# Query norms ahead of the turn, the causal mask as a product, and scores in two rings of banks

## The chip, the cores and the metric

One Trainium2 chip, one core of it. The metric is the device time of one launch in microseconds (us). Engines: PE is TensorE (matrix products into PSUM banks), DVE is VectorE, ACT is ScalarE, POOL is GpSimd, and SP issues most of the transfers.

## The reference

One transformer block on 256 tokens of width 2048, fp32 throughout. What matters here is the mixer's attention half: 8 query heads of 128 in 2 groups, each group sharing one key and value head.

```python
q = rope(rms_norm(q.reshape(B, S, NSA_HEADS, dh), q_norm_g), pos)
...
p_c = masked_softmax(jnp.einsum('bgsrd,bgcd->bgsrc', q, kc) * scale, mask_c)      # compressed, 15 blocks
...
p = masked_softmax(jnp.einsum('bgqrd,bgqkd->bgqrk', q_i, kg) * scale, mask)       # selected
...
p_w = masked_softmax(jnp.einsum('bgnqrd,bgnkd->bgnqrk', qw, kband) * scale, mask_w)  # window
...
return gates[..., 0:1] * o_cmp + gates[..., 1:2] * o_slc + gates[..., 2:3] * o_win
```

At 256 tokens there are four blocks to select from and 16 may be selected, and the window is 512 long, so the selected and the window branch are both plain causal attention, with keys of their own. The other half of the mixer is a gated linear recurrence (`rglru_branch`); after the mixer come an output projection and a PEER feed-forward that reads all 16384 experts.

## The kernel before

The kernel runs in three parts. The first (up to about 205 us) computes the modulation rows and most of the input projection. The second (about 205 to 365 us) finishes the projection and does the whole mixer. The third is the output projection (to 475 us) and the feed-forward (to the end).

All weights are streamed through four buffers of 1 MB (`raw`); each piece is split into a high and a low fp32r half (`split`: ACT line 209 casts, DVE line 210 subtracts), and three fp32r products stand for one fp32 product (`mm3`, lines 358 to 360). Besides, DVE works off rows of the modulation weights (`ada`, line 231, tile `av`, two buffers of 1 MB while the mixer runs), and PE takes others of them as products (`adp_item`, line 271).

The second part is a set of Python generators, `PROG` (line 57), that `mix` steps in turn: `q`/`e` evacuate a projected block (`ev_q`, `ev_kv`, `ev_rnn`), `b` and `l` are projection blocks (tiles `r` and `xg`), `c` is the compression, `r0` to `r3` are the four groups of the recurrence, `s0` to `s3` are the scores of group g = i // 2 and token block tb = i % 2, and `o0` to `o3` the outputs. The order in the program is a priority: a scheduler places each instruction in its engine's queue, and each engine then runs its queue in order.

`scores` works on one head a step, with n = 128 keys for tb = 0 and 256 for tb = 1, both branches side by side in one PSUM bank. PE makes two fp32 products (line 811). DVE scales by the query's norm out of PSUM into the tile `pt` (line 802, tb = 1 only, the part without mask), scales and masks the diagonal part (line 803), and takes the row maximum (line 806). ACT takes the exponential in place in `pt` and sums it (line 795). The score bank is free after lines 802 and 803. The norms `rq` come from `ev_q`, which turns the unnormed queries at once (line 641) and works out the norm beside that (lines 642, 643).

PSUM has one ring of four banks (`ps_x`, also called `PO`: projection blocks and attention outputs), one of three (`ps_t`, also `ps_a`: transposes, scores, recurrence gates) and one of one bank. The recurrence keeps one set of tiles `u`, `ta`, `ti`; PE's gates `rp` (line 756) wait for the convolution on DVE (line 751).

Of the kernel before, what the change touches and what calls it, by code (L numbers as in the profile page):

```python
# [7 lines left out]
F32 = mybir.dt.float32  # L8
F32R = mybir.dt.float32r
U32 = mybir.dt.uint32  # L10
I32 = mybir.dt.int32
AF = mybir.ActivationFunctionType
OP = mybir.AluOpType
AX = mybir.AxisListType

P = 128
# [3 lines left out]
NT = S // P  # L20
HD = 128
NH = 8
NG = 2
# [39 lines left out]
SCALE = HD ** -0.5  # L63
# [7 lines left out]
def kernel(  # L71
# [40 lines left out]
    ps_a = ps_t  # L112
    PO = ps_x
# [470 lines left out]
    kT = zp.tile([P, 2, NG, S], F32, name="kT")  # L584
    vv = zp.tile([P, NT, 2, NG, HD], F32, name="vv")
    gates = zp.tile([P, NT, 24], F32, name="gates")
    rq = zp.tile([P, NT, NH], F32, name="rq")
    kcT = zp.tile([P, 32], F32, name="kcT")
    vc = zp.tile([16, NG, HD], F32, name="vc")

    win = oT.rearrange("p h t -> p (h t)").rearrange("p (a l g n) -> p a l g n", a=2, l=32, g=2)
    ckT = xgT.rearrange("p h t -> p (h t)")[:, 0:4 * S].rearrange("p (a g t) -> p a g t", a=2, g=2)
    V.memset(win[:, :, :, :, NCMP:16], 0.0)
# [29 lines left out]
    def transpose4(zr, name):  # L623
        tp = ps_t(f"tp_{name}")
        for h in range(4):
            T.transpose(tp[:, h * P:(h + 1) * P], zr[:, h * P:(h + 1) * P], ident)
        return tp
# [4 lines left out]
    def ev_q(j, pst):  # L632
        tab = table(0)
        s = tp1.tile([P, NT, 4], F32, tag="ssq", bufs=2, name=f"ssq{j}")
        z = []
        for tb in range(NT):
            z.append(zrow(tp1, f"q{j}{tb}"))
            sumsq(s[:, tb], pst[tb], 4, f"q{j}{tb}")
            rope(z[tb], pst[tb], 4, tab[:, tb, 0], tab[:, tb, 1], f"q{j}{tb}")
            yield  # L640
        tp = transpose4(z[0], f"q{j}0")
        r = rsqrt(tp1, s.rearrange("p b h -> p (b h)"), HD, 8, f"q{j}")
        V.tensor_scalar(rq[:, :, 4 * j:4 * j + 4], r.rearrange("p (b h) -> p b h", b=NT), SCALE, None, OP.mult)
        yield
        A.copy(qT[:, 4 * j:4 * j + 4, tbs[0]], tp.rearrange("p (h t) -> p h t", h=4))
        tp = transpose4(z[1], f"q{j}1")
        yield
        A.copy(qT[:, 4 * j:4 * j + 4, tbs[1]], tp.rearrange("p (h t) -> p h t", h=4))
# [90 lines left out]
    def recurrence(gr):  # L739
        n = RG  # L740
        if True:
# [18 lines left out]
                A.activation(ta[:, c_], ta[:, c_], AF.Tanh, scale=spl[:, k:k + 1], bias=spl[:, k:k + 1])  # L760

            d = xr[:, :, 0:S]
            V.tensor_scalar(d, d, 0.5, 0.5, OP.mult, OP.add)
            V.scalar_tensor_tensor(out=u, in0=ti, scalar=1.0, in1=u, op0=OP.add, op1=OP.mult)
            yield
            V.scalar_tensor_tensor(out=ti, in0=ta, scalar=1.0, in1=d, op0=OP.add, op1=OP.mult)
            A.activation(ta, ta, AF.Sqrt)
            yield
            V.scalar_tensor_tensor(out=d, in0=ti, scalar=2.0, in1=d, op0=OP.subtract, op1=OP.mult)
            V.tensor_scalar(ti, d, -2.0, -1.0, OP.mult, OP.add)  # L770
            yield
            V.tensor_tensor(u, u, d, OP.mult)
            yield
            V.scalar_tensor_tensor(out=u, in0=ta, scalar=-1.0, in1=u, op0=OP.mult, op1=OP.mult)
            yield
            for i in range(n):
                V.tensor_tensor_scan(d[:, i], ti[:, i], u[:, i], 0.0, OP.mult, OP.add)
# [5 lines left out]
    def scores(sp, g, tb):  # L783

        n = (tb + 1) * P
        sums = sp.tile([P, 4, 2], F32, tag=f"sums{tb}", bufs=1, name=f"sums{tb}{g}")
        pts = [sp.tile([P, 2, n], F32, tag=f"pt{tb}", bufs=4, name=f"pt{tb}{g}{hh}") for hh in range(4)]
        m2 = sp.tile([P, 4, 2], F32, tag=f"m2{tb}", bufs=1, name=f"m2{tb}{g}")
        held[g, tb] = sums, pts
        scs = {}  # L790
        for i in range(6):
            if 0 <= i - 2:
                hh = i - 2
                for br in range(2):
                    A.activation(pts[hh][:, br], pts[hh][:, br], AF.Exp, bias=m2[:, hh, br:br + 1],
                                 accum_out=sums[:, hh, br:br + 1])
            if 0 <= i - 1 < 4:
                hh = i - 1
                s3 = scs.pop(hh)[:, 0:2 * n].rearrange("p (b n) -> p b n", b=2)
                r1 = rq[:, tb, 4 * g + hh:4 * g + hh + 1]  # L800
                if tb == 1:
                    V.tensor_scalar(pts[hh][:, :, 0:P], s3[:, :, 0:P], r1, None, OP.mult)
                V.scalar_tensor_tensor(
                    out=pts[hh][:, :, n - P:n], in0=s3[:, :, n - P:n], scalar=r1,
                    in1=caus.unsqueeze(1).to_broadcast([P, 2, P]), op0=OP.mult, op1=OP.add)
                V.tensor_reduce(m2[:, hh], pts[hh], AX.X, OP.max, negate=True)
            if i < 4:
                h = 4 * g + i
                scs[i] = ps_a(f"sc{tb}{h}")
                for br in range(2):  # L810
                    T.matmul(scs[i][:, br * n:(br + 1) * n], qT[:, h, tbs[tb]], kT[:, br, g, 0:n], start=True, stop=True)
            yield

    def outputs(sp, g, tb):
# [12 lines left out]
        for hh in range(4):  # L827
# [3 lines left out]
        cm = con[:, C_CMP + 16 * tb:C_CMP + 16 * tb + 16].unsqueeze(1).to_broadcast([P, 4, 16])  # L831
        va = con[:, C_VAL + 16 * tb:C_VAL + 16 * tb + 16].unsqueeze(1).to_broadcast([P, 4, 16])
        mx = sp.tile([P, 4], F32, tag="cmx", bufs=2, name=f"cmx{g}{tb}")
        V.tensor_tensor(pc, cps[:, 0:64].rearrange("p (h n) -> p h n", h=4),
                        rq[:, tb, hs].unsqueeze(2).to_broadcast([P, 4, 16]), OP.mult)
        V.tensor_tensor(pc, pc, cm, OP.add)
        V.tensor_reduce(mx, pc, AX.X, OP.max)
        V.tensor_tensor(pc, pc, mx.unsqueeze(2).to_broadcast([P, 4, 16]), OP.subtract)
        A.activation(pc, pc, AF.Exp)
# [600 lines left out]
```

## Time and profile before

| | us |
|---|---|
| median of 3 runs | 2024.65 (2024.57 to 2025.96) |
| the profiled execution | 2027.09 |
| its span in the trace | 2025.3 |
| PE busy in the span | 1953.6 (96%) |
| DVE busy | 1529.3 (76%) |
| ACT busy | 1024.1 (51%) |

The profiled execution took 1.8 us more than its span and 2.4 us more than the median. The shares are means over parts with different limits: after 475 us PE is busy all the time, before that it is not.

### The profile page before, as it was taken

To read this page: it belongs to the slowest core of one execution; us is meant where nothing else is said; L and a number is where in the kernel's file an instruction comes from. 1 tells how busy PE (TensorE), PEld (TensorE's weight loads), DVE (VectorE), ACT (ScalarE), POOL (GpSimd) and SP (SyncE) were. 2 spreads that over 40 slices of the span, in tenths; PEclk is the share of its full clock that TensorE was granted. 3 is DMA by queue.
4 is the path that set the end of the run, shared out by engine and by line. 5 is a ranking of instruction groups with operands and counts; after the bars stand their busy time and mean duration, and the time that the engine had idled before them with its cause. 6 is when DMAs were issued, how large, how long until landed. Compare 5 with 4: busy or idle time off the path is not lost.

```text
span 2025.3 us, 30935 instructions
## 1 busy us (share of the span) xinstructions
PE 1953.6 (96%) x12346; PEld 1728.4 (85%) x12346; DVE 1529.3 (76%) x2342; ACT 1024.1 (51%) x1519; POOL 67.6 (3%) x107
## 2 busy tenths in 40 slices
PE   5999898898999999999999999999999999999998
PEld 4777565787999999999998888888899999999997
DVE  7888999887999888788757666666566666665566
ACT  3544676455445767677654444444344444444442
POOL 0000000000000000000011000000000000000000
PEclk7999998898999999999999999999999999999999
DMA  9898778895546676666798776775577777676563
GB/s 374 325 372 330 277 307 315 345 347 219 175 169 208 215 260 234 229 230 232 270 331 300 246 242 229 234 251 201 190 267 253 262 250 253 240 243 212 190 223 131
DMA packets 77600, 515.39 MB, mean 254 GB/s; under 512 B 8720, under 2 KB 9232, under 8 KB 21904
## 3 DMA queue, kind: packets, MB, share of 16 engines
q1 hardware_dynamic: 63792, 450.50, 62.0%
q0 software_dynamic: 13664, 62.92, 9.0%
q8 instruction: 96, 1.57, 0.3%
q14 instruction: 48, 0.39, 0.1%
HBM read 481.93 MB, written 31.46 MB: 253 GB/s over the span
## 4 chain that ended last, share of the span: by engine, by line
PE 75%; DVE 10%; issue 10%; DMA 3%; ACT 2%; POOL 1%; SPq 0%; DVEq 0%; POOLq 0%
PE u L359 11%; PE u L358 11%; PE u L360 11%; PE d L377 8%; PE d L376 8%; PE d L375 8%; DVE av L231 3%; DVE wl L210 3%; PE wq L375 2%; PE wq L376 2%; PE wq L377 2%; PE y L360 1%; PE y L358 1%; PE y L359 1%; DMA wd<-stg 1%
## 5 line engine op out<-in xcount | busy, mean ns | idle before, releaser
L210 DVE TENSOR_TENSOR wl<-raw,wh 128x1024 fp32r<-128x1024 f32 x649 | 789.3, 1220 | 374.7 <-ACT wh L209 372.0
L209 ACT CAST wh<-raw 128x1024 fp32r<-128x1024 f32 x649 | 680.2, 1051 | 768.5 <-PE u L360 364.2
L377 PE MATMUL d<-xH,wl 128*128 128x256 f32 x2048 | 568.4, 278 | 0.8 <-DVE wl L210 0.7
L375 PE MATMUL d<-xH,wh 128*128 128x256 f32 x2048 | 568.4, 278 | 0.0
L376 PE MATMUL d<-xL,wh 128*128 128x256 f32 x2048 | 567.9, 277 | 0.0
L359 PE MATMUL u<-wl,ah 128*128 128x512 f32 x1024 | 398.9, 390 | 1.3 <-DVE wl L210 1.3
L358 PE MATMUL u<-wh,ah 128*128 128x512 f32 x1024 | 398.7, 389 | 0.0
L360 PE MATMUL u<-wh,al 128*128 128x512 f32 x1024 | 398.4, 389 | 0.0
L377 PEld LDWEIGHTS d<-xH,wl 128*128 128x128 f32 x2048 | 385.3, 188 | 1.3 <-DVE wl L210 1.2
L376 PEld LDWEIGHTS d<-xL,wh 128*128 128x128 f32 x2048 | 385.2, 188 | 0.4
L375 PEld LDWEIGHTS d<-xH,wh 128*128 128x128 f32 x2048 | 385.2, 188 | 0.4
L359 PEld LDWEIGHTS u<-wl,ah 128*128 128x128 f32 x1024 | 192.2, 188 | 41.2 <-DVE wl L210 1.7
L360 PEld LDWEIGHTS u<-wh,al 128*128 128x128 f32 x1024 | 192.3, 188 | 40.2
L358 PEld LDWEIGHTS u<-wh,ah 128*128 128x128 f32 x1024 | 192.2, 188 | 39.7
L231 DVE SCALAR_TENSOR_TENSOR av<-av,cb 128x2048 f32<-128x2048 f32 x64 | 145.8, 2283 | 6.0 <-DMA av<-in_ada_w_dram 6.0
L1198 DVE TENSOR_TENSOR oh<-con,idT 128x1024 fp32r<-128x1024 f32 x64 | 78.1, 1221 | 33.4 <-PE w L1218 33.3
L1228 ACT ACTIVATE ga<-oh,gh 128x128 fp32r<-128x128 f32 x256 | 83.0, 394 | 18.1 <-DVE oh L1198 16.3
L375 PE MATMUL wq<-xH,wh 128*128 128x256 f32 x256 | 73.5, 288 | 2.5 <-ACT xH L209 2.5
L376 PE MATMUL wq<-xL,wh 128*128 128x256 f32 x256 | 73.2, 286 | 0.0
L377 PE MATMUL wq<-xH,wl 128*128 128x256 f32 x256 | 73.0, 285 | 0.0
L1284 DVE TENSOR_TENSOR acc<-acc,u 128x512 f32<-128x512 f32 x112 | 71.5, 679 | 0.0
L1210 DVE TENSOR_TENSOR stg<-stg,w 128x256 f32<-128x256 f32 x128 | 48.3, 421 | 10.3 <-ACT stg L1209 10.3
(363 smaller groups left out, 2080.0 us busy)
## 6 DMA issues: line engine op xcount, KB each, us to landing
raw<-in_down_dram SPq DMA_DIRECT2D x128, 1024.0 KB, 5.6
raw<-in_up_dram SPq DMA_DIRECT2D x128, 1024.0 KB, 5.4
av<-in_ada_w_dram SPq DMA_DIRECT2D x64, 1024.0 KB, 7.1
raw<-in_w_a_dram SPq DMA_DIRECT2D x32, 1024.0 KB, 9.0
raw<-in_ada_p_dram SPq DMA_DIRECT2D x16, 1024.0 KB, 7.1
raw<-in_w_out_dram SPq DMA_DIRECT2D x16, 1024.0 KB, 8.1
raw<-in_wq_dram SPq DMA_DIRECT2D x16, 1024.0 KB, 5.2
wd<-stg POOLq DMA_DIRECT2D x8, 2048.0 KB, 8.4
```

The costliest lines, as they stand in the source:

```text
L209: A.copy(dst_h, src)
L210: V.tensor_tensor(dst_l, src, dst_h.bitcast(F32), OP.subtract)
L231: V.scalar_tensor_tensor(out=t, in0=t, scalar=1.0, in1=cb, op0=OP.mult, op1=OP.mult, accum_out=m)
L358: T.matmul(o, ah, bh, start=first, stop=False)
L359: T.matmul(o, ah, bl, start=False, stop=False)
L360: T.matmul(o, al, bh, start=False, stop=last)
L375: T.matmul(o, wh[:, kk, ws], bH[:, kc], start=f and i % 2 == 0, stop=False)
L376: T.matmul(o, wh[:, kk, ws], bL[:, kc], start=False, stop=False)
L377: T.matmul(o, wl[:, kk, ws], bH[:, kc], start=False, stop=e and i % 2 == 1)
L1198: V.tensor_tensor(oh, iota.unsqueeze(1).unsqueeze(1).to_broadcast([P, 4, 2, P]), idT[:, 4 * q:4 * q + 4].unsqueeze(3).to_broadcast([P, 4, ...
L1228: A.activation(ga[:, k, 0], hot[:, k], AF.Copy, scale=gh[:, t:t + 1].bitcast(F32))
L1284: V.tensor_tensor(a, a, pst[tb], OP.add)
```

## The change

Five edits. The queries are multiplied by their norm and by the scale on DVE, in rows, ahead of the transposes, so that the scores come out of PE final. The causal mask is a third product into the score bank: identity (fp32r) times the mask (fp32r), 256 columns. Scores of even heads use the ring of three, those of odd heads the ring of four; DVE's maximum and ACT's exponential both read the bank, and `pt` is written by the exponential alone. In the recurrence one DVE operation (line 763) becomes an ACT Identity with bias 1, with the constants after it adjusted. In the compressed branch the multiplication by the norm (line 834) goes. `rq` is dropped, and `vc` moves into a part of `xgT`.

```diff
+    idr = zp.tile([P, P], F32R, name="idr")
+    car = zp.tile([P, P], F32R, name="car")
+    A.copy(idr, ident)
+    A.copy(car, caus)
...
-    vc = zp.tile([16, NG, HD], F32, name="vc")
+    vc = xgT[0:16, 6].rearrange("p (g d) -> p g d", g=NG)
...
+        r = rsqrt(tp1, s.rearrange("p b h -> p (b h)"), HD, 8, f"q{j}")
+        V.tensor_scalar(r, r, SCALE, None, OP.mult)
+        yield
+        for tb in range(NT):
+            z4 = z[tb].rearrange("p (h d) -> p h d", h=4)
+            V.tensor_tensor(z4, z4, r[:, 4 * tb:4 * tb + 4].unsqueeze(2).to_broadcast([P, 4, HD]), OP.mult)
         tp = transpose4(z[0], f"q{j}0")
-        r = rsqrt(tp1, s.rearrange("p b h -> p (b h)"), HD, 8, f"q{j}")
-        V.tensor_scalar(rq[:, :, 4 * j:4 * j + 4], r.rearrange("p (b h) -> p b h", b=NT), SCALE, None, OP.mult)
...
-            V.tensor_scalar(d, d, 0.5, 0.5, OP.mult, OP.add)
+            A.activation(d, d, AF.Identity, bias=1.0)
...
-        for i in range(6):
-            if 0 <= i - 2:
-                hh = i - 2
+        for i in range(5):
+            if i:
+                s3 = scs.pop(i - 1)
                 for br in range(2):
-                    A.activation(pts[hh][:, br], pts[hh][:, br], AF.Exp, bias=m2[:, hh, br:br + 1],
-                                 accum_out=sums[:, hh, br:br + 1])
-            if 0 <= i - 1 < 4:
-                hh = i - 1
-                s3 = scs.pop(hh)[:, 0:2 * n].rearrange("p (b n) -> p b n", b=2)
-                r1 = rq[:, tb, 4 * g + hh:4 * g + hh + 1]
-                if tb == 1:
-                    V.tensor_scalar(pts[hh][:, :, 0:P], s3[:, :, 0:P], r1, None, OP.mult)
-                V.scalar_tensor_tensor(
-                    out=pts[hh][:, :, n - P:n], in0=s3[:, :, n - P:n], scalar=r1,
-                    in1=caus.unsqueeze(1).to_broadcast([P, 2, P]), op0=OP.mult, op1=OP.add)
-                V.tensor_reduce(m2[:, hh], pts[hh], AX.X, OP.max, negate=True)
+                    A.activation(pts[i - 1][:, br], s3[:, br], AF.Exp, bias=m2[:, i - 1, br:br + 1],
+                                 accum_out=sums[:, i - 1, br:br + 1])
             if i < 4:
                 h = 4 * g + i
-                scs[i] = ps_a(f"sc{tb}{h}")
+                s3 = (PO if i % 2 else ps_a)(f"sc{tb}{h}")[:, 0:2 * n].rearrange("p (b n) -> p b n", b=2)
+                scs[i] = s3
                 for br in range(2):
-                    T.matmul(scs[i][:, br * n:(br + 1) * n], qT[:, h, tbs[tb]], kT[:, br, g, 0:n], start=True, stop=True)
+                    T.matmul(s3[:, br], qT[:, h, tbs[tb]], kT[:, br, g, 0:n], start=br == 0, stop=False)
+                T.matmul(s3[:, :, n - P:n], idr, car.unsqueeze(1).to_broadcast([P, 2, P]), start=False, stop=True)
+                V.tensor_reduce(m2[:, i], s3, AX.X, OP.max, negate=True)
...
-        V.tensor_tensor(pc, cps[:, 0:64].rearrange("p (h n) -> p h n", h=4),
-                        rq[:, tb, hs].unsqueeze(2).to_broadcast([P, 4, 16]), OP.mult)
-        V.tensor_tensor(pc, pc, cm, OP.add)
+        V.tensor_tensor(pc, cps[:, 0:64].rearrange("p (h n) -> p h n", h=4), cm, OP.add)
```

## Rows read from the trace of the kernel before

**Rows 1.** Windows by part: busy us of each engine, clock, DMA share, GB/s.

```profile
205.00:365.00 160.00, 140.96 (x831) 92.92 (x829) 151.06 (x368) 105.49 (x243) 2.83 (x4) 0.92 0.78 299
365.00:475.00 110.00, 102.01 (x468) 83.32 (x468) 97.05 (x133) 53.82 (x77) 4.35 (x8) 0.93 0.89 341
475.00:2025.30 1550.30, 1536.25 (x10326) 1412.69 (x10326) 1112.01 (x1627) 772.70 (x1066) 59.39 (x89) 1.00 0.67 231
```

**Rows 2.** Windows inside the mixer, same columns (PE, PEld, DVE, ACT, POOL).

```profile
241.00:260.00 19.00, 17.77 (x202) 14.13 (x202) 19.00 (x48) 14.73 (x46) 0.00 (x0) 1.00 0.67 241
260.00:296.00 36.00, 35.63 (x188) 21.97 (x189) 32.25 (x83) 24.65 (x49) 0.00 (x0) 0.95 0.80 317
304.00:329.00 25.00, 18.30 (x103) 11.43 (x101) 24.97 (x60) 16.00 (x49) 0.00 (x0) 0.82 0.80 311
329.00:365.00 36.00, 30.04 (x140) 19.74 (x140) 32.58 (x65) 21.84 (x36) 2.83 (x4) 0.83 0.83 318
```

**Rows 3.** The chain that ended last, 205 to 380 us: start, us, what.

```profile
237.55 0.60 DVE zr_q L616
...
303.99 0.34 DVE xrT L763
...
311.59 0.40 DVE pt L802
311.99 0.39 DVE pt L803
...
322.99 0.13 DVE pc L838
...
328.98 3.75 PE rp L756 x8
...
345.44 0.43 PE xg L359
345.87 0.23 PE xg L360
```

**Rows 4.** PE and DVE in order of time; idle before and its releaser in brackets.

```profile
260.11 0.41 PE L711 MATMUL cmpt<-con,zr_cc 128*128 128x32 f32 x2 [1.00 <-ACT zr_cc L709]
261.66 0.30 PE L360 MATMUL gl<-xH,wl 128*24 128x256 f32 x1 [0.26 <-DVE wl L210]
274.94 1.97 PE L756 MATMUL rp<-u,lw 128*128 128x256 f32 x8
328.98 3.75 PE L756 MATMUL rp<-u,lw 128*128 128x256 f32 x8 [6.29 <-DVE u L751]
...
224.04 0.69 DVE L547 TENSOR_TENSOR part<-r,part 128x512 f32<-128x512 f32 x1 [0.67 <-PE r L360]
225.84 1.22 DVE L210 TENSOR_TENSOR wl<-raw,wh 128x1024 fp32r<-128x1024 f32 x1 [0.71 <-ACT wh L209]
323.83 2.28 DVE L231 SCALAR_TENSOR_TENSOR av<-av,cb 128x2048 f32<-128x2048 f32 x1
```

**Rows 5.** Groups of 205 to 350 us: busy us, mean ns, idle before.

```profile
L547 DVE TENSOR_TENSOR part<-r,part 128x512 f32<-128x512 f32 x8 | 5.3, 680 | 0.7 <-PE r L360 0.7
L772 DVE TENSOR_TENSOR u<-u,xrT 128x512 f32<-128x512 f32 x4 | 2.7, 682 | 0.0
L767 ACT ACTIVATE ta<-ta 128x512 f32<-128x512 f32 x4 | 2.5, 632 | 1.7 <-DVE ti L766 1.7
```

**Rows 6.** Window of the feed-forward: 256-column fp32r products back to back.

```profile
500.00:550.00 50.00, 50.00 (x429) 50.00 (x428) 45.68 (x220) 22.33 (x26) 0.00 (x0) 1.00 0.50 170
```

**Rows 7.** `av` loads: transfers (median us to landing), SP's issues; ACT's table loads.

```profile
av<-in_ada_w_dram SPq DMA_DIRECT2D x19, 1024.0 KB, 4.9
...
317.30 4.37 SPq L222 DMA_DIRECT2D av<-in_ada_w_dram  x2
...
250.67 1.28 ACT L767 ACT_TABLE_LOAD   x1
252.62 1.28 ACT L795 ACT_TABLE_LOAD   x1
```

More of the change, by code (lines that the diff above doesn't have):

```diff
@@ L586 @@
     gates = zp.tile([P, NT, 24], F32, name="gates")
-    rq = zp.tile([P, NT, NH], F32, name="rq")
+    idr = zp.tile([P, P], F32R, name="idr")
+    car = zp.tile([P, P], F32R, name="car")
+    A.copy(idr, ident)
+    A.copy(car, caus)
     kcT = zp.tile([P, 32], F32, name="kcT")
-    vc = zp.tile([16, NG, HD], F32, name="vc")
+    vc = xgT[0:16, 6].rearrange("p (g d) -> p g d", g=NG)
     win = oT.rearrange("p h t -> p (h t)").rearrange("p (a l g n) -> p a l g n", a=2, l=32, g=2)
@@ L768, in recurrence @@
             yield
-            V.scalar_tensor_tensor(out=d, in0=ti, scalar=2.0, in1=d, op0=OP.subtract, op1=OP.mult)
-            V.tensor_scalar(ti, d, -2.0, -1.0, OP.mult, OP.add)
+            V.scalar_tensor_tensor(out=d, in0=ti, scalar=4.0, in1=d, op0=OP.subtract, op1=OP.mult)
+            V.tensor_scalar(ti, d, -0.5, -1.0, OP.mult, OP.add)
             yield
@@ L773, in recurrence @@
             yield
-            V.scalar_tensor_tensor(out=u, in0=ta, scalar=-1.0, in1=u, op0=OP.mult, op1=OP.mult)
+            V.scalar_tensor_tensor(out=u, in0=ta, scalar=-0.25, in1=u, op0=OP.mult, op1=OP.mult)
             yield
```

## The prediction

> **What bounds the kernel now.** I read the windows by part first. After 475 us PE is busy in 1536 of 1550 us, so the change, which lies wholly before, can only shift that part as a block. The output projection from 365 to 475 us is also PE's (102 of 110). In the mixer, 205 to 365 us, DVE is busy in 151 of 160 us and PE in 141 [rows 1]. All the edits lie there, and there the finer windows tell two kinds of stretches apart. From 241 to 260 us both are full (DVE 19.0 of 19, PE 17.8), and from 260 to 296 PE is (35.6 of 36) while DVE has 3.7 us to spare. From 304 to 329 us it is the other way round: DVE 24.97 of 25, PE 18.3, ACT 16.0, and the granted clock falls to 0.82 on average [rows 2]. So DVE time taken out before 304 us is worth little, and DVE time taken out after it is worth nearly its whole length.
>
> The chain that ended last then says the same of single operations: from 304 to 329 us it runs over DVE's scalings, maxima and recurrence steps, and after that over PE's `rp` [rows 3]. PE in order of time shows the handover: `rp` of the last recurrence group starts at 328.98 us after 6.29 us of idle time, released by `u`, line 751, on DVE [rows 4].
>
> **Part by part.** Durations overlap by some hundredths, so I price DVE by the steps of the chain, which are what one operation holds the engine for.
>
> Scores, DVE. Line 802 holds it 0.40 us, line 803 0.39 [rows 3]. Four heads of each tb = 1 block lose both, four of each tb = 0 block lose line 803. For `s0` and `s1` (241 to 260 us): 4 x 0.40 + 8 x 0.39 = 4.7 us. For `s2` and `s3` (304 to 329 us) the same 4.7.
>
> The maximum now reads PSUM. No maximum from PSUM stands in the trace; the nearest rows are two-operand operations of 512 columns, one with an operand in PSUM (line 547, 680 ns) and one wholly in SBUF (line 772, 682 ns) [rows 5]. I price the move at nothing; the other bound would be the whole of such a difference, also nothing. [...]
>
> Recurrence, line 763: 0.34 us less on DVE for each group [rows 3], so 0.34 in each of the two stretches. Its place is taken by an ACT operation on 512 columns, nearest row 632 ns (line 767) [rows 5]. It is covered by ACT's spare 9 us of 25 in the later stretch; without that cover it would cost its 0.6 us.
>
> Compressed branch, line 834: two of its four instructions fall into 304 to 329 us, at 0.13 us a step (line 838, of the same tile) [rows 3]: 0.26 us.
>
> Query norms. Four multiplications of 128x512 are added, two per half of the heads, nearest step 0.60 us (line 616) [rows 3]. The first two (1.2 us) fall at about 219 us. DVE waits there for PE and for ACT, 0.67 and 0.71 us [rows 4], which covers them. What they delay is late for nothing before the scores at 241 us, since DVE's next work in priority is at hand; uncovered they cost 1.2 us. The second two fall among `s0` and `s1`, from which I take them: 4.7 + 0.34 - 1.2 = 3.9 us less on DVE there. The queries of the second half are needed only by `s3`, some 50 us later.
>
> Mask products, PE: 16, of 256 columns, fp32r, eight in each stretch. Back to back such products take 50 / 429 = 0.117 us [rows 6], the lower bound. Upper bound: the first fp32r product after fp32 ones steps 0.43 us where the next steps 0.23, for 512 columns [rows 3], so I bound it by 0.43. In most places a score product is followed by an fp32r product anyway, so one such step is mostly there already; I take 0.20, nearer the low end: 1.6 us in each stretch.
>
> Copies of identity and mask, 128 columns on ACT, come once at the beginning of the mixer, in ACT's free third [rows 1]: nothing. No transfer is added or moved.
>
> Now what of this lies on the path.
> - First stretch, to 296 us. PE is the limit. What DVE and ACT can give back is the time PE waited for them at its end: 1.00 us (the copy `zr_cc`, behind the exponentials on ACT) and 0.26 us [rows 4]. Against that, 1.6 us of mask: 1.6 - 1.26 = +0.3 us. The rest of DVE's 3.9 us becomes idle time.
> - Second stretch. DVE loses 4.7 + 0.34 + 0.26 = 5.3 us. PE's idle 6.29 us shrinks by 1.6 us of mask to 4.7, which is all that `rp` can come earlier: -4.7 us. From there on everything follows PE.
> - Clock. `rp` (eight products) takes 3.75 us after the idle time [rows 3], against 1.97 at 274.94 us [rows 4]. If the shorter gap holds the clock, 1.8 us come back. The rows don't settle whether it does, so I take less than half: -0.8 us.
>
> Sum: +0.3 - 4.7 - 0.8 = -5.2 us. Against the profiled execution's own 2027.09 us (1.8 above its span) that is 2021.9; that execution stands 2.4 us above the median, so for the median 2024.65 - 5.2, say **2019.5 us**.
>
> **The rivals.**
> - *The bank waits for ACT (slower).* Before, a score bank was free as soon as DVE had scaled it. Now it is held to the end of the exponential. ACT has a stretch without exponentials among `s0` and `s1`: it loads a table for Sqrt at 250.67 us and one back for Exp at 252.62, until 253.90, so 3.2 us [rows 7]. If a score product at the head of PE's queue meets no free bank then, the projection products behind it wait too, on the engine that is full there. For it: PE runs its queue in order, and PE is full. Against it: two rings (three banks and what the projection leaves of four) instead of one of three. Price: +3.2 +0.3 in the first stretch; the same pair of loads beside `s3` takes 3.2 us, and with 1.6 us of mask that uses up the 4.7 us gained there; a clock that falls again, another 1.8 us: +5.3, **2030 us**. It decides from a wait of PE for a bank of about 4 us together.
> - *The `av` rows cap the gain (same).* The `av` product of 323.83 us [rows 4] uses a buffer whose load was issued at 317.30 and takes 4.9 us to land [rows 7]: it is there at 322.2, only 1.6 us early. DVE's queue is in order, so if the products keep their places, what is saved behind that load's issue is lost to its landing. Then only what `s3` saves counts, 4 x 0.79 + 0.34 = 3.5 us, less the 0.3: **2021.5 us**. Against it: only some 1.4 us (three times line 803 and the two of line 834) lie behind the issue.
> - *The queries' rows are held (same).* The two row buffers that the queries take are freed only after the norm is worked out, about 3 us later than now; the keys' rows use the same two. If DVE finds nothing to fill with, 1.2 us of multiplication and up to 2 us of waiting go onto DVE's chain of 224 us, and the gain shrinks to about 2 us: **2022.5 us**. For it: DVE's next steps there are the keys'. Against it: keys are wanted at 241 us only.
>
> **How the numbers follow.** Something within 0.2% (4.05 us, 2020.6 to 2028.7) is about what a measurement of this kernel can't tell from no change. The forecast, with or without its clock term, sits at the edge: I give it and better packings 0.56. The two capped cases get 0.16 and 0.10, the bank 0.18. So faster 0.56, same 0.26, slower 0.18. The likeliest's own range goes from 2017.2 (masks at 0.117, 0.94 us a stretch: -0.3 in the first, -5.3 in the second, the clock held, -1.8) to 2024 (masks at 0.43, 3.4 us a stretch: +2.2, -2.9, no clock). Below, two `av` products of 2.28 us each [rows 4] that leave the chain in another packing would give 2012.7; above stands the bank. The whole range is 2014 to 2028, which leaves out about 2 in 10.
>
> **What would show it.** Right: DVE busy time in the mixer down by 9 us (151 to 142); lines 802, 803, 763 gone; `rp` of the last group released after 2 us of idle time or less; output projection some 5 us earlier. The mask at about 0.2 us a product. Wrong, if a score product on PE waits for an exponential on ACT (the bank), if DVE is idle for an `av` load near 320 us, or if keys' rows wait near 218 us. Also wrong if the scheduler puts an `av` product ahead of a maximum at another place than now: each is 2.28 us on the chain [rows 4].

## The result, and the profile after

The changed kernel takes 2036.75 us in the median of 5 runs (2032.77 to 2040.36), the kernel before 2025.96 in 5 runs beside it (2024.57 to 2030.08). The ratio is 1.0053, with a 95% interval of 1.0036 to 1.0069: slower by about 11 us, where 5 us less were forecast, and outside the range. The profiled execution took 2040.36 us, its span is 2038.6. Single executions of one kernel lie up to some 18 us apart in these runs (and one of e11's twelve took 2197.93 us, a slow one that is in no ratio), so times are told by medians and ratios, and a profile is used for where a wait lies.

The windows by part of the changed kernel, which answer to [rows 1] (start and end, then busy us of PE, PEld, DVE, ACT, POOL, then clock, DMA share, GB/s):

```profile
205.00:365.00 160.00, 140.98 (x816) 95.12 (x814) 137.51 (x319) 99.38 (x248) 0.00 (x0) 0.91 0.73 277
365.00:475.00 110.00, 100.00 (x482) 82.15 (x475) 93.03 (x129) 56.38 (x77) 6.11 (x10) 0.92 0.92 351
475.00:2038.60 1563.60, 1541.49 (x10367) 1415.31 (x10365) 1126.84 (x1657) 779.83 (x1077) 60.53 (x91) 1.00 0.67 231
```

DVE is busy 13.5 us less in 205 to 365 us, as the edit meant, and PE has been busy no longer. The transfers have done less: 277 GB/s against 299. Finer windows of the changed kernel, the last one of a stretch where the output projection should be running:

```profile
240.00:260.00 20.00, 10.09 (x53) 6.96 (x52) 15.95 (x35) 6.85 (x25) 0.00 (x0) 0.74 0.66 256
260.00:300.00 40.00, 38.69 (x321) 26.53 (x320) 31.09 (x78) 31.85 (x78) 0.00 (x0) 0.96 0.70 264
304.00:329.00 25.00, 18.99 (x74) 13.23 (x74) 23.11 (x43) 19.21 (x54) 0.00 (x0) 0.80 0.79 298
329.00:365.00 36.00, 36.00 (x186) 23.38 (x184) 29.98 (x53) 18.50 (x34) 0.00 (x0) 1.00 0.76 285
365.00:385.00 20.00, 10.88 (x64) 8.95 (x57) 15.41 (x36) 12.10 (x18) 2.84 (x4) 0.66 1.01 409
```

and the same view of the kernel before, first and last stretch:

```profile
240.00:260.00 20.00, 17.77 (x202) 14.13 (x202) 20.00 (x49) 14.73 (x46) 0.00 (x0) 1.00 0.66 232
365.00:385.00 20.00, 19.63 (x90) 16.47 (x91) 15.45 (x30) 8.68 (x12) 0.00 (x0) 0.84 0.95 367
```

Two holes stand out. At 240 to 260 us PE is busy for 10.1 us instead of 17.8, and ACT for 6.9 instead of 14.7. At 365 to 385 us PE is busy for 10.9 instead of 19.6 at a clock of 0.66. Much of the second hole is a shift: the step from the attention's norm (tile `nha`) to the output projection (tile `y`), in which PE waits for DVE and ACT, lay at 353.0 to 365.4 us and lies now at 366.8 to 381.2. The DMA engines are full in it (1.01), but none of PE's waits there is for a load. In 304 to 329 us, where the gain was to come from, PE is busy for hardly more than before (18.99 against 18.30 in [rows 2]). PE's waits of the changed kernel, 205 to 390 us (what waited, for what; us in all, times, longest):

```profile
PE tp_q L630 <- DVE zr_q L650: 5.0, 1, 5.0
PE adp L271 <- DMA raw<-in_ada_p_dram: 4.9, 1, 4.9
PE rbta L892 <- DVE rsr_nha L413: 4.8, 1, 4.8
PE y L358 <- ACT xH L209: 3.6, 1, 3.6
PE xg L358 <- ACT pt L803: 3.4, 1, 3.4
PE rp L764 <- DVE u L759: 2.6, 2, 2.3
```

The same view of the kernel before, 200 to 400 us, has three of these tiles:

```profile
PE y L358 <- ACT xH L209: 3.6, 1, 3.6
PE rbta L893 <- DVE rsr_nha L413: 2.7, 1, 2.7
PE adp L271 <- DMA raw<-in_ada_p_dram: 1.3, 1, 1.3
```

So `tp_q` and `xg` are the new waits, `adp` and `rbta` (the norm behind `nha`) are longer ones, and `y` is as it was. The line of `rp` is not the wait that was to shrink. Its 2.3 us belong to the third group of the recurrence, and the last group's products come without a wait (PE in order of time):

```profile
308.22 1.13 PE L764 MATMUL rp<-u,lw 128*128 128x256 f32 x4 [2.31 <-DVE u L759]
...
338.73 1.89 PE L764 MATMUL rp<-u,lw 128*128 128x256 f32 x8
```

The mark of 2 us or less is met, and the eight products take 1.89 us instead of 3.75. But they start 9.7 us later than before, not 4.7 us earlier: the time in which PE waited for `u` is now filled with `xg`.

The first new wait is at the turn of the queries; all engines of the changed kernel in order of time:

```profile
244.08 0.17 DVE L407 TENSOR_SCALAR rsv_q<-ssq 128x8 f32<-128x8 f32 x1
...
247.80 1.70 PE L271 MATMUL adp<-raw,cs 128*32 128x512 f32 x8 [4.87 <-DMA raw<-in_ada_p_dram]
...
250.42 0.16 DVE L412 TENSOR_TENSOR rst_q<-rst_q,rsv_q 128x8 f32<-128x8 f32 x1
250.50 2.28 DVE L231 SCALAR_TENSOR_TENSOR av<-av,cb 128x2048 f32<-128x2048 f32 x1
...
252.71 0.16 DVE L413 SCALAR_TENSOR_TENSOR rsr_q<-rst_q,rsr_q 128x8 f32<-128x8 f32 x1
...
253.71 1.29 DVE L650 TENSOR_TENSOR zr_q<-zr_q,rsr_q 128x512 f32<-128x512 f32 x2
254.55 1.94 PE L630 MATMUL tp_q<-con,zr_q 128*128 128x128 f32 x8 [5.05 <-DVE zr_q L650]
255.67 0.59 ACT L653 COPY qT<-tp_q 128x512 f32<-128x512 f32 x1 [11.63 <-PE tp_q L630]
```

The norm is 13 short steps on [128, 8], each waiting for the one before. The scheduler fills the gaps between them with whatever is ready, and an `av` product is 2.28 us long. So the 13 steps of 0.16 us last from 244.08 to 253.7. In the kernel before it was stretched in the same way (241.1 to 250.8), but nothing waited for it: the turn had gone ahead. Now the transposes `tp_q` stand behind it in PE's queue, and the copy `qT` in ACT's, which stands still for 11.63 us with all exponentials and casts behind it. The other half of PE's hole is the `adp` row of the fence: PE ended the `adp` products before them at 242.9 us, the load for these went out at 243.0, and they stood at the head of PE's queue.

The second new wait is at `xg`, the projection block. The chain that ended last in the changed kernel, at 317 us (start, us, what):

```profile
317.09 1.28 ACT L775
...
318.38 0.63 ACT ta L775
...
319.03 1.28 ACT L803
...
320.33 0.57 ACT pt L803 x2
...
320.94 0.79 PE xg L358
```

`xg` needs two banks of the ring of four, and odd heads of `s2` and `s3` hold them until their exponentials are done. ACT does a Sqrt in between, with a table load of 1.28 us before and one after it. `xg` starts at 320.9 us; before, it started at 288.4 and 75 of its 96 products (lines 358 to 360) had run by 321 us, in part in time in which PE now stands still. In the changed kernel one had, PE is busy for only 14.9 of 20 us at 300 to 320 us, and the other 95 come on top of the work behind: PE is busy in all 36 us of 329 to 365. The loads behind `xg`'s weights are late too. SP's first load of the output projection, before

```profile
337.54 0.38 SPq L204 DMA_DIRECT2D raw<-in_w_out_dram  x1
```

and in the changed kernel:

```profile
362.36 1.13 SPq L204 DMA_DIRECT2D raw<-in_w_out_dram  x2
```

The delay along the way, by the start of each tile's first product (last one for `tp_q` and `po`), in the two profiles:

| | `tp_c` | `tp_q` last | `gl` | `xg` | `rp`, last group | `po` last | `nha` | `y` | `wq` |
|---|---|---|---|---|---|---|---|---|---|
| before | 207.0 | 241.7 | 261.0 | 288.4 | 329.0 | 344.8 | 353.0 | 365.4 | 475.1 |
| after | 210.4 | 256.1 | 273.7 | 320.9 | 338.7 | 354.5 | 366.8 | 381.2 | 490.9 |
| later by | 3.4 | 14.4 | 12.7 | 32.5 | 9.7 | 9.7 | 13.8 | 15.8 | 15.8 |

The first 3.4 us are not put down to the edits: `tp_c` starts at 207.2 to 210.4 us in the profiles of the sixteen kernels below, and at 208.2 in e15 and e16, where nothing ahead of it was changed. Over them, the turn is 11 us late; at the last `rp` and at the end of the outputs, `po`, only 6.3 are left, so the mixer did win some of it back; `nha` waits for more projection work and is 10.4 late, and the output projection 12.4, since the norm behind `nha` is 2.1 us longer. The output projection itself takes what it took before, 109.7 us to `wq`, so the late `w_out` loads cost nothing that this profile shows.

### The profile page after: what moved, and what is told of

It is laid out like the page before. It is cut to its first block, busy times and chain, and to the rows that moved or that the text cites. A ratio compares the mean times of both kernels' runs of the same rounds, so it can differ in the third digit from the quotient of the medians.

```text
span 2038.6 us, 30949 instructions
## 1 busy us (share of the span) xinstructions
PE 1955.4 (96%) x12362; PEld 1730.8 (85%) x12362; DVE 1523.1 (75%) x2314; ACT 1024.6 (50%) x1525; POOL 67.6 (3%) x107
## 4 chain that ended last, share of the span: by engine, by line
PE 78%; DVE 10%; issue 6%; DMA 3%; ACT 3%; POOL 1%; SPq 0%; DVEq 0%; POOLq 0%
PE u L359 11%; PE u L358 11%; PE u L360 11%; PE d L377 9%; PE d L375 9%; PE d L376 9%; DVE av L231 3%; DVE wl L210 2%; PE wq L375 1%; PE wq L376 1%; PE wq L377 1%; PE y L359 1%; PE y L360 1%; PE y L358 1%; DMA wd<-stg 1%
```

## The experiments

Sixteen kernels, each run beside the kernel before on the same chip. "Ring" is the ring of four banks for odd heads.

| run | norm | ring in | `xg` starts | `wq` starts | ratio to before, 95% |
|---|---|---|---|---|---|
| after | ahead | both groups | 320.9 | 490.9 | 1.0053 (1.0036 to 1.0069) |
| e1 | ahead | none (old scores) | 298.6 | 484.0 | 1.0038 (1.0021 to 1.0054) |
| e2 | late | both | 315.1 | 491.9 | 1.0075 (1.0049 to 1.0101) |
| e3 | ahead | none | 298.6 | 486.8 | 1.0028 (1.0013 to 1.0043) |
| e4 | ahead | both | 316.6 | 487.0 | 1.0072 (1.0045 to 1.0099) |
| e5 | late | none | 291.6 | 480.6 | 1.0023 (1.0003 to 1.0044) |
| e6 | old | both (old scores) | 305.2 | 478.6 | 1.0021 (1.0006 to 1.0037) |
| e7 | ahead | first | 292.0 | 477.8 | 1.0011 (0.9994 to 1.0029) |
| e8 | ahead, turn later | none | 302.4 | 487.9 | 1.0074 (1.0052 to 1.0097) |
| e9 | ahead, short | first | 295.4 | 481.4 | 1.0023 (1.0008 to 1.0038) |
| e10 | late | first | 287.1 | 480.8 | 1.0017 (1.0003 to 1.0030) |
| e11 | old | none (old scores) | 289.4 | 477.1 | 1.0009 (0.9995 to 1.0023) |
| e12 | ahead | both, `l0` ahead | 292.8 | 481.2 | 1.0046 (1.0028 to 1.0064) |
| e13 | ahead | second | 315.4 | 485.4 | 1.0063 (1.0041 to 1.0085) |
| e14 | ahead | first, `l0` ahead | 292.2 | 482.9 | 1.0050 (1.0031 to 1.0068) |
| e15 | old | none (old scores) | 288.1 | 483.4 | 1.0066 (1.0043 to 1.0089) |
| e16 | old | none (old scores) | 289.9 | 474.6 | 0.9965 (0.9946 to 0.9985) |

`xg` and `wq` are told from one profile each, the ratios from all executions. What lies behind `wq`, where no kernel has an edit, took 1543.6 (e13) to 1556.8 us (e7) in these profiles. Even so the ratios mostly go with `wq`, which starts at 475.1 us before: up to 1.0028 it starts by 481.4 us, except in e3, and from 1.0038 on later than that, except in e12. So most of the loss arises ahead of `wq`.

### Norm and rings, one at a time (e1 to e4)

e1 is the kernel before with the norm ahead of the turn alone:

```diff
-        tp = transpose4(z[0], f"q{j}0")
         r = rsqrt(tp1, s.rearrange("p b h -> p (b h)"), HD, 8, f"q{j}")
-        V.tensor_scalar(rq[:, :, 4 * j:4 * j + 4], r.rearrange("p (b h) -> p b h", b=NT), SCALE, None, OP.mult)
+        V.tensor_scalar(r, r, SCALE, None, OP.mult)
+        yield
+        for tb in range(NT):
+            z4 = z[tb].rearrange("p (h d) -> p h d", h=4)
+            V.tensor_tensor(z4, z4, r[:, 4 * tb:4 * tb + 4].unsqueeze(2).to_broadcast([P, 4, HD]), OP.mult)
+        tp = transpose4(z[0], f"q{j}0")
...
-                r1 = rq[:, tb, 4 * g + hh:4 * g + hh + 1]
+                r1 = ones[:, 0:1]
```

> The kernel before with one edit alone: the queries multiplied by their norm ahead of the turn. DVE's scaling of the scores stays, with a factor of one, so its cost is unchanged; masks, banks and recurrence are those of before. Theory 1 (the turn): the transposes of the second half of the queries now stand behind the norm's chain of some 13 dependent DVE operations, and PE's and ACT's queues stand behind the transposes; that alone costs 8 to 11 us, time 2033 to 2037, and PE shows a wait of 5 us or more for the normed rows. Theory 2 (the bank): the loss is the score bank held until ACT's exponential, so this edit costs only its 2.4 us of DVE time, 2026 to 2029.

1.0038, as the first theory said. The hole is there by this edit alone (PE and ACT in order of time):

```profile
245.86 0.79 PE L359 MATMUL r<-wl,xH 128*128 128x512 f32 x1 [5.53 <-DVE wl L210]
...
252.84 0.59 ACT L648 COPY qT<-tp_q 128x512 f32<-128x512 f32 x1 [11.02 <-PE tp_q L625]
```

ACT waits for the turn, as in the changed kernel. PE's 5.5 us were expected to be a wait for the normed rows; they are one for `wl`, a split that DVE does between the norm's steps. And the last group's `rp` waits only 2.3 us here for `u` (PE is busy for 2.33 of 5 us at 335 to 340), though e1 saves DVE nothing: it starts at 337.9 us, later than before. So a shorter wait there is no sign of saved DVE time.

e2 is the changed kernel with the norm late: the scale of the exponential, and a product of 128x2 for the maximum.

```diff
+                                 scale=rq[:, tb, 4 * g + i - 1:4 * g + i], accum_out=sums[:, i - 1, br:br + 1])
...
+                V.tensor_scalar(m2[:, i], m2[:, i], rq[:, tb, h:h + 1], None, OP.mult)
```

> The changed kernel with the norm taken off the queries again: they are turned at once as before, the mask is still a product, both rings are used, and the norm enters as the scale of ACT's exponential and as one DVE multiplication of the negated maximum (128x2) per head; the compressed branch keeps its multiplication by the norm. Theory 1 (the turn): the loss goes, and of the 9 us of DVE time that the change saves something stays: 2019 to 2026. Theory 2 (the bank): the banks are held as in the changed kernel, so it stays at 2033 to 2038.

1.0075: no gain at all, so the turn alone is not the cause. `xg` starts at 315.1 us here too, after 3.62 us of waiting for `pt` on ACT. e3 keeps the norm ahead and puts all scores into the ring of three:

```diff
-                s3 = (PO if i % 2 else ps_a)(f"sc{tb}{h}")[:, 0:2 * n].rearrange("p (b n) -> p b n", b=2)
+                s3 = ps_a(f"sc{tb}{h}")[:, 0:2 * n].rearrange("p (b n) -> p b n", b=2)
```

> The changed kernel with all scores in the ring of three banks, so that the ring of four is left to the projection blocks. Theory 1 (the turn): PE and ACT still wait for the normed rows; 2032 to 2038, within 3 us of the changed kernel. Theory 2 (the bank): the projection block no longer waits for an exponential (3.4 us at 321 us in the changed kernel, and a lower clock after it); 2025 to 2030.

1.0028, `xg` at 298.6 us. The median of 2034.08 us is what the first theory expected, above the 2025 to 2030 of the second. e4 moves the recurrence edit back to DVE (`V.tensor_scalar(d, d, 1.0, None, OP.add)` for the Identity):

> The changed kernel with the recurrence's added operation back on DVE (adding 1 there, the changed constants kept). Theory 1 and theory 2: neither speaks of it; within 2 us of the changed kernel, 2034 to 2039. Theory 3 (ACT's chain): the Identity on ACT, 0.5 us on the chain in three of the four groups, behind gates and exponentials in ACT's queue, is what costs: 2 us or more faster than the changed kernel.

1.0072, so that edit is not the loss.

### The later `xg` (e6, e7, e13, e12, e14)

e6 is the kernel before with `scs[i] = (PO if i % 2 else ps_a)(...)` and nothing else.

> The kernel before with odd heads' scores in the ring of four and nothing else. Theory (the later scores take the banks of xg): first product of xg at 310 us or later (288 before), PE idle at 300 to 320 us, 4 to 8 us slower than before. Rival (the ring hurts only where the bank is also held to the exponential, which it is not here): xg before 300 us, within 3 us of before.

`xg` at 305.2 us, after a wait of 2.83 us for line 803 on DVE, and 1.0021 (some 4 us). That lies between the two expectations: with the bank free after the scaling, as before, `xg` is less late and the loss is smaller. e7 is the changed kernel with `(PO if i % 2 and g == 0 else ps_a)`, e13 the one with `g == 1`.

> The changed kernel with odd heads in the ring of four only for the first group of heads (s0, s1); s2 and s3 in the ring of three. Theory: the loss by the second ring sits in s2 and s3, so xg starts before 302 us, as in the run with one ring, and the time is that run's within 3 us: 2031 to 2037 us beside about 2027 before. Rival (the ring's cost sits in the first group): xg at 315 us or later, 2036 us or more.

> The complement of the run with the second ring in the first group: the changed kernel with odd heads in the ring of four only in s2 and s3. Nothing is left out. Theory (the later group's odd heads keep xg out of its banks, and that is the larger part of the loss): xg starts at 310 us or later, ratio 1.004 or more. Rival (the loss needs both groups, or sits elsewhere): xg before 302 us, or 1.003 or less.

The group that keeps the ring decides. Products of `xg` by its tile, in e7 (count, ns, first and last start, shape):

```profile
L358 PE MATMUL xg<-wh,xH x32: 387/393/504, 292.0 to 351.3; 128*128 128x512 f32 x32
```

and in e13:

```profile
L358 PE MATMUL xg<-wh,xH x32: 389/389/500, 315.4 to 356.7; 128*128 128x512 f32 x32
```

1.0011 against 1.0063, and the intervals lie apart. By 321 us e7 has run 62 of the 96 `xg` products and e13 20, where the changed kernel has run one. What that means for PE at 300 to 320 us shows in the windows of the changed kernel

```profile
300.00:320.00 20.00, 14.94 (x64) 8.84 (x62) 18.93 (x32) 14.24 (x26) 0.00 (x0) 0.91 0.82 308
```

and of e7:

```profile
300.00:320.00 20.00, 20.00 (x97) 16.21 (x95) 19.83 (x29) 17.13 (x42) 0.00 (x0) 1.00 0.80 307
```

Note that e7 keeps the whole hole at the turn (4.8 us for `zr_q`, 11.6 on ACT) and still comes out within what can't be told from no change.

e12 keeps both rings and puts `l0` ahead of `s3` and `s2` in `PROG`; e14 does that to e7.

```diff
-PROG = 'q0 b0@.2 e0,k0,k1,p0 b1@.4 e1,b2,e2 s0|s1|r0,c0,b3 c1,g0@.2 e3 o0|o1|r1@.3 r2 s3@.25 s2 l0@.25 o2|o3|r3,l1@.3'
+PROG = 'q0 b0@.2 e0,k0,k1,p0 b1@.4 e1,b2,e2 s0|s1|r0,c0,b3 c1,g0@.2 e3 o0|o1|r1@.3 r2 l0@.25 s3@.25 s2 o2|o3|r3,l1@.3'
```

> The changed kernel with both rings, and the projection block xg (l0) put ahead of s3 and s2 in the order of the program instead of behind them. Nothing is left out. Theory (with both rings the odd heads' banks keep xg out): xg starts before 305 us and has its two banks first, the time comes down to that of the second ring in the first group only, ratio 1.000 to 1.002 where the change as it stands gave 1.005. Rival (the ring of four is simply too busy): the odd heads now wait for the two banks that are left, a wait of PE for pt of 3 us or more between 295 and 330 us, 1.004 or more.

> The run with the second ring in the first group only, with l0 (xg) ahead of s3 and s2 in the program. xg is early with or without this order. If the order itself costs: 1.003 to 1.005, as with both rings in this order (1.0046), and then that run says nothing against the theory of the late xg. If the order is free: 1.000 to 1.002 as in the old order, and then the second ring costs s2 and s3 time in another way than by a late xg.

`xg` is early in e12 (292.8) and the loss is still 1.0046; but e14, which has no ring in the second group, loses 1.0050 by the new order alone. So the order costs by itself. With `xg` ahead of the scores the ring in the second group adds nothing (e14 to e12), with `xg` behind them it adds 0.4% (e7 to the changed kernel). That fits a ring that costs by holding `xg` up; that the loss by the order hides one by the ring isn't excluded.

### The turn again (e5, e8, e9, e10)

e5 is e2 with one ring, e10 is e2 with the ring in the first group only.

> The changed kernel with both suspects taken out: norm applied late (scale of the exponential, one small DVE product for the maximum), all scores in the ring of three; mask product, maximum from the bank and recurrence edit stay. Two mechanisms (turn behind the norm, and the projection block's banks): no gap of PE over 3 us at 240 to 256 us, first product of xg between 288 and 300 us, 2019 to 2028 us in all. Rival, the bank that is held up to the exponential, or the mask product, is what costs: score products wait for ACT by several us, 2034 us or more.

1.0023, or 2031.5 us where 2019 to 2028 were expected. No wait of PE at the turn above 1.8 us, `xg` early, but a score product now waits for the bank that the exponential holds, 3.4 us (e5's PE in order of time):

```profile
257.27 2.08 PE L807 MATMUL sc<-kT,qT 128*128 128x256 f32 x4 [3.41 <-ACT pt L800]
```

> The changed kernel with both waits taken out and the second ring kept where it does not meet xg: norm late (scale of the exponential, a small DVE product for the maximum), odd heads in the ring of four for s0 and s1 only. Nothing is left out. Theory (the two waits are the whole loss, and the ring of three alone held scores up by 3.4 us in the first group): no wait of PE over 2 us at 240 to 260 us, xg before 296 us, ratio 0.996 to 1.000. Rival (maximum and exponential from the bank, the mask and the small products cost as much as the scalings that they replace): 1.001 to 1.003, as with one ring.

1.0017, in the rival's range: the two waits are not the whole loss. No wait of PE at the turn above 1.2 us, `xg` at 287.1, the bank's wait gone, and still not faster than before: now `rp` waits 5.1 us for DVE. Counted from `tp_c`, e10's output projection starts when it did before (158.5 us against 158.4), and it takes 113.2 us to `wq` instead of 109.7; why was not found. e8 evacuates and turns the second half's queries one part later (`b2 s0|s1|r0,c0,b3 e2` in place of `b2,e2 s0|s1|r0,c0,b3`).

> The run with one ring again, and the second half's queries are evacuated and turned one part later in the program (behind s0, s1, r0, c0 and b3 instead of ahead of them), so that nothing of these parts stands behind them in priority. Nothing is left out. Theory (PE and ACT queues stood behind the turn): the gap of PE at 240 to 256 us goes, 2020 to 2029 us. Rival (it is the added DVE work, or the chain is as long wherever it stands): a gap of 4 us or more behind the turn at another place, 2032 us or more.

1.0074: the wait for `zr_q` is gone, but PE stands 7.4 us for an `adp` load and 4.7 us at `ptt`, which is the rival's gap at another place. e9 is e7 with one Newton step instead of three for these queries (`steps=3 - 2 * j`).

> The run with the second ring in the first group only, with one Newton step instead of three in the norm of the second half's queries (this norm is less exact; nothing else is left out). DVE's queue then holds six short steps and one av product of 2.3 us fewer between the row sums and the two multiplications. Theory (PE's and ACT's queues stand behind that chain): the wait of tp_q for zr_q shrinks from 4.8 us to 2 us or less, ACT's from 11.6 to 9 or less, and up to 3 us come off: ratio 0.997 to 1.0005 where three steps gave 1.0011. Rival (the wait is hidden: PE would have stood for the loads of adp anyway, 4.9 us): same wait for adp, same ratio as with three steps, 1.0005 to 1.002.

The wait shrank as the theory said (e9's waits of PE):

```profile
PE adp L271 <- DMA raw<-in_ada_p_dram: 4.8, 1, 4.8
...
PE tp_q L630 <- DVE zr_q L650: 1.6, 1, 1.6
```

ACT's went from 11.6 to 8.3 us, and the time didn't follow: 1.0023 where e7 had 1.0011, intervals overlapping. The rival holds here: 3 us less at the turn are worth nothing that these runs can measure.

### Is DVE the price at all? (e11, e15, e16)

e11 takes work from DVE in the kernel before, in the stretch that the prediction held to be DVE's:

```diff
...
-                V.tensor_reduce(m2[:, hh], pts[hh], AX.X, OP.max, negate=True)
+                if g:
+                    V.tensor_scalar(m2[:, hh], pts[hh][:, :, 0], 0.0, None, OP.mult)
+                else:
+                    V.tensor_reduce(m2[:, hh], pts[hh], AX.X, OP.max, negate=True)
...
-            V.tensor_scalar(pts[hh][:, 0], pts[hh][:, 0], cf[:, hh, 0:1], None, OP.mult)
+            if not g:
+                V.tensor_scalar(pts[hh][:, 0], pts[hh][:, 0], cf[:, hh, 0:1], None, OP.mult)
```

> The kernel before with some 5 us less DVE work in s2, s3, o2 and o3 and no other edit: the maxima of the second group become a 128x2 product with zero (4 x 0.25 and 4 x 0.51 us less), and the multiplications of line 828 of the second group are left out (2.5 us). So this softmax has no maximum taken off (its exponent is scaled by 1/64 instead), and the first branch's gate factor of these heads is missing. The prediction's premise (DVE time taken out after 304 us is worth nearly its whole length): 4 to 6 us faster than before, ratio 0.997 to 0.998, first w_out load issued earlier. Rival (the stream of weights and the background products set the end of this stretch, and DVE time is not the price): within 1.5 us of before, ratio 0.9993 to 1.001, first w_out load no earlier.

1.0009: nothing gained, and the first `w_out` load goes out at 347.4 us, not earlier than before. Part of where the time went shows in the costliest DVE group of 300 to 330 us. In the kernel before (busy us, mean ns, idle):

```profile
L231 DVE SCALAR_TENSOR_TENSOR av<-av,cb 128x2048 f32<-128x2048 f32 x4 | 9.1, 2280 | 0.0
```

in e11:

```profile
L231 DVE SCALAR_TENSOR_TENSOR av<-av,cb 128x2048 f32<-128x2048 f32 x5 | 11.4, 2283 | 0.0
```

and of the changed kernel:

```profile
L231 DVE SCALAR_TENSOR_TENSOR av<-av,cb 128x2048 f32<-128x2048 f32 x6 | 13.7, 2284 | 0.0
```

Freed time is filled with background rows. In e11 `rp` still waits 4.8 us for `u`, but it starts 2.7 us earlier than before, and the outputs end 3.1 us earlier. What was won up to there is lost behind it, for a good part by an `av` product among the short steps of the norm behind `nha` (e11's DVE and PE in order of time; PE's wait was 2.7 us before):

```profile
355.82 0.16 DVE L412 TENSOR_TENSOR rst_nha<-rst_nha,rsv_nha 128x2 f32<-128x2 f32 x1
355.90 2.28 DVE L231 SCALAR_TENSOR_TENSOR av<-av,cb 128x2048 f32<-128x2048 f32 x1
...
359.59 0.45 PE L897 MATMUL rbta<-con,rsr_nha 128*128 128x128 f32 x1 [4.81 <-DVE rsr_nha L413]
```

The starts in this and the next two kernels, each from one profile:

| | `tp_c` | `rp`, last group | `po` last | `nha` | `y` | `wq` |
|---|---|---|---|---|---|---|
| before | 207.0 | 329.0 | 344.8 | 353.0 | 365.4 | 475.1 |
| e11 | 207.7 | 326.3 | 341.7 | 351.2 | 365.6 | 477.1 |
| e15 | 208.2 | 320.0 | 334.0 | 358.1 | 373.6 | 483.4 |
| e16 | 208.2 | 321.0 | 335.5 | 344.7 | 360.1 | 474.6 |

e15 and e16 cut these rows themselves: 12 `av` products take 64 columns, and in e16 their loads too.

```diff
...
+        w = 64 if lite.get(id(t), (False,))[0] else D
-        V.scalar_tensor_tensor(out=t, in0=t, scalar=1.0, in1=cb, op0=OP.mult, op1=OP.mult, accum_out=m)
+        V.scalar_tensor_tensor(out=t[:, 0:w], in0=t[:, 0:w], scalar=1.0, in1=cb[:, 0:w], op0=OP.mult,
+                               op1=OP.mult, accum_out=m)
```

> The kernel before, where 12 of the av products between about 280 and 360 us take 64 columns instead of 2048 (their modulation values are wrong by that); their loads stay. Some 25 us of DVE work go from the stretch that the prediction held to be DVE's. Rival of the prediction's own kind (DVE time is the price there): 5 us or more faster, 0.9975 or less. Theory (the stream of weights sets when the output projection runs, whatever DVE does): the mixer ends earlier, w_out loads hardly do, at most 3 us faster, 0.9985 or more.

> As the run with the small av products, and the loads of these 12 rows also bring 64 columns only (11.6 MB less; modulation values wrong in the same way). Theory (stream): w_out loads are issued and land earlier, DMA share below 0.9 at 365 to 385 us, 4 us or more faster than with the products cut alone. Rival (DVE or PE is the price): within 2 us of that run.

With some 25 us of DVE work gone (an estimate, from 12 products of 2.28 us; DVE is busy for 120.0 us of 205 to 365, 151.1 before) and all transfers kept, the outputs end 10.8 us earlier, and the kernel is slower, 1.0066. At 330 to 365 us of e15 DVE is all but idle and the DMA engines are not (the window):

```profile
330.00:365.00 35.00, 24.36 (x111) 14.12 (x108) 5.53 (x24) 8.19 (x13) 0.00 (x0) 0.76 0.86 345
```

SP's queue of e15 in order of time says what they carry:

```profile
333.21 11.75 SPq L224 DMA_DIRECT2D av<-in_ada_w_dram  x5
345.05 0.86 SPq L199 DMA_DIRECT2D raw<-in_ada_p_dram  x2
```

With the products cut to 64 columns five `av` loads of 1 MB go out in a row, in 11.75 us, where the kernel before issued two (332.33 us, 5.11 us), and the `adp` rows that PE needs next are issued only behind them, at 345.05: PE's longest wait for one is 9.3 us, until 352.1. e15's loss is thus a wait of its own, more than was expected of either theory. With the loads cut as well, PE waits 1.0 us for `adp` rows, and the output projection starts at 360.1 us. PE is busy all through 365 to 385 us, though at a clock of 0.63 and with 75 products where there were 90, and the DMA share there is 0.50, where it was 0.95 before (windows of e16):

```profile
330.00:365.00 35.00, 26.31 (x129) 17.18 (x127) 16.82 (x52) 17.61 (x27) 2.84 (x4) 0.77 0.71 268
365.00:385.00 20.00, 20.00 (x75) 17.28 (x74) 10.09 (x16) 5.62 (x7) 0.00 (x0) 0.63 0.50 166
```

0.9965, a whole per cent under e15: with the DVE work gone, the transfers make this difference. How much of the 0.35% under the kernel before is theirs and how much DVE's is not separated, and the profile doesn't show where it comes from: it is of an execution of 2025.5 us, where the median is 2019.0, and `wq` starts only 0.5 us earlier there.

## Why the prediction was wrong

**The failed step.** "DVE time taken out after it is worth nearly its whole length", and with it "From there on everything follows PE". The first was read from DVE being busy in 24.97 of 25 us and from the chain running over it [rows 2, 3]. Inside the mixer it was right in part: in e11 some 5 us less DVE work bring the last `rp` 2.7 us and the outputs 3.1 us forward, in e15 25 us bring them 9.0 and 10.8. Beyond the outputs it failed: e11's output projection starts 0.2 us later than before, e15's 8.2. Behind the outputs the time follows the norm behind `nha`, in which an `av` product took the time back, and PE's next loads. And 9.1 us of DVE's work at 300 to 330 us were background `av` rows, which take any time that is free: in the changed kernel they went from 4 to 6, 4.6 us more, against the 5.3 us that the sum had credited. The 4.7 us of PE's idle time were no gain either: in the changed kernel it is filled with `xg`, and the last `rp` starts 9.7 us later.

**What the sum left out: `xg`.** The bank rival had the mechanism, ACT's two table loads around a Sqrt, but expected a score product to stand for it and the projection products only behind that. It was the projection block itself that stood: it needs two of the four banks and comes behind `s2` and `s3` in the program. e7 against e13 shows the group and the size, 1.0011 against 1.0063, and e7 against the changed kernel 1.0011 against 1.0053. The row of the wait is 3.4 us only. The rest, as the profiles have it, is that `xg`'s products had in part filled time in which PE had nothing else, and now come on top of the work behind. How the loss divides between this and the loads behind `xg`'s weights was not tested. In the four runs that start `xg` after 315 us (after, e2, e4, e13) the first `w_out` load goes out at 359 to 362 us and the ratio is 1.0053 to 1.0075; in the others it goes out at 339 to 354 us, with ratios up to 1.0074, and no order among these.

**"The queries of the second half are needed only by `s3`."** They are needed by `s2` too, and by the compressed branch of their group, but `s3` is the first. As a need of data it is nearly right, but in these profiles each engine takes its queue in order, and the transposes (PE waits 5.05 us for them) and their copies (ACT, 11.63 us) hold up what stands behind them. Only the multiplications were priced, as DVE time, and the latency of the norm's 13 steps ahead of them was put at nothing: 9.6 us. e1 shows the hole and a loss of 0.38% for this edit alone. That the same hole costs something in the changed kernel is not shown: with it e7 is at 1.0011, without it e10 at 1.0017, and with a shorter one e9 at 1.0023.

**Terms that held, and one that was small.** DVE fell by 13.5 us in 205 to 365 us (9 forecast; the rest would be work that moved beyond 365). The mask product was too cheap: 0.20 to 0.40 us from its start to the next product's where PE doesn't wait behind it (14 of 16), 0.29 in the mean against 0.20 forecast, inside the bounds; 16 of them are 1.5 us over the sum. The Identity on ACT took its 632 ns without a wait of its own. Maximum and exponential out of the bank, in the changed kernel (busy us, mean ns, idle):

```profile
L812 DVE TENSOR_REDUCE m<-sc 128x2 f32<-128x512 f32 x8 | 5.4, 682 | 1.0 <-PE sc L811 1.0
L812 DVE TENSOR_REDUCE m<-sc 128x2 f32<-128x256 f32 x8 | 3.3, 418 | 4.9 <-PE sc L811 4.9
```

Out of SBUF, in the kernel before, the same two took 674 and 408 ns:

```profile
L806 DVE TENSOR_REDUCE m<-pt 128x2 f32<-128x512 f32 x8 | 5.4, 674 | 0.0
L806 DVE TENSOR_REDUCE m<-pt 128x2 f32<-128x256 f32 x8 | 3.2, 408 | 0.0
```

They are 0.01 us apart, nothing, as priced.

**Where the expected gain went, and what stays open.** With the ring kept out of the second group the change is at 1.001 to 1.003 (e3, e5, e7, e9, e10), not under 1. Freed DVE time goes into `av` rows; these can lengthen a norm's chain (e11: PE waits 4.8 us for the norm behind `nha`, 2.7 before), and 1 MB loads that go out sooner can hold up the weights (e15 against e16: PE's waits for `adp` loads 10.8 and 1.0 us, the first `w_out` load issued at 347.4 and 339.0). That either is the whole remainder in e5 or e10 was not shown; in e10 it lies in the output projection. Open too: whether e1 alone costs more than e3, which contains it (1.0038 and 1.0028, the intervals overlap), why `l0` ahead of the scores costs 0.4% (e14), and why the output projection takes from 108.0 (e5) to 114.5 us (e16). No version here beat the kernel before without leaving work out.

## What to carry to other kernels

An engine that limits a stretch need not limit the time: subtract the work that only fills gaps, take a few us out as a test, and follow what is won to the end of the chain (3 us at the outputs, nothing at the output projection). A wait that gets shorter is no gain by itself, since the engine may only come later or do other work in it (the changed kernel's last `rp` comes without the wait of 6.29 us, and 9.7 us later). When a tile moves to another ring, list who else takes banks from that ring and stands later in the program: a block that had filled idle time comes on top of the work behind when it starts late (95 of `xg`'s 96 products, at 321 us). A dependent chain of short steps is as long as what the scheduler puts between them (here 2 us of work in 9.6), so a step that in-order queues wait for (ACT's stood 11.63 us) shouldn't follow one.

## What was not expected of the hardware

An engine made faster made the kernel slower by the transfers it set off: with 25 us less DVE work five 1 MB loads were issued in a row at 333 us, and PE stood 9.3 us for the next load that it needed (e15, 1.0066), where the same kernel with these loads cut to 64 columns was 0.35% faster than the kernel before (e16).
